# Seven block products for eight in the first MLP GEMM, with the activations of the MLP kept in DRAM and w_out run by halves of the tokens

## The chip, the cores and the metric

The kernel runs on one core of one Trainium2 chip. A core has a matrix engine (TensorE, PE in the profile; its weight loads are listed apart as PEld), three engines for elementwise work (VectorE or DVE, ScalarE or ACT, GpSimd or POOL), SyncE (SP), which here issues nearly all DMA transfers, and 16 DMA engines. The metric is the time of one execution on the device in microseconds; lower is better. A run gives several such times, and the median is used.

## The reference

One decoder layer is applied to 1024 prompt tokens and 32 decode tokens, 1056 in all. Everything ahead of the MLP (two attention-like branches and their merge) is the same before and after the change. What matters here is the end of the layer:

```python
y = (jax.nn.sigmoid(ga) * ya + jax.nn.sigmoid(gb) * yb) @ w_out
x = x + gt_m * rmsnorm(y, g_post_mix)

h2 = rmsnorm(x, g_pre_mlp) * (1 + sc_f) + sh_f
u = jnp.square(jax.nn.relu(h2 @ w_up))
x = x + gt_f * rmsnorm(u @ w_down, g_post_mlp)
```

The model width is 1024 and the MLP width 4096, so `w_up` is 1024 x 4096 and `w_down` 4096 x 1024. All values are float32, and the vectors `gt_m`, `sc_f`, `sh_f`, `gt_f` differ between the prompt and each of the 8 decode sequences.

## The kernel before, in words

All activations are kept channel-major: a tile has 128 channels on the partitions and tokens along the free axis. A float32 operand of a GEMM is split into two rounded parts, high and low, and a product is three matmuls for each block of 128 input channels: high weight x high activation, high x low, low x high (lines 400 to 402, in the helper `gemm`). They accumulate in one PSUM bank for one block of 128 output channels and one chunk of 352 tokens; three chunks make up the 1056 tokens (`CH`, line 26). Weights arrive by DMA as `wr`, and ACT makes the high part `wh` (line 261), DVE and POOL in turn the low part `wl` (line 262), for 128 x 1024 values at a time.

The last GEMM before this part is the second projection of the merge (`merge_b`). Its eviction writes the merged activations as high and low parts into `MG`, a pair of tiles for each chunk of 352 tokens.

Then `w_out` runs chunk by chunk. Each of its 8 blocks of output channels is copied out of PSUM by ACT (line 1289), squared by ACT (line 1294) and summed by POOL (line 1295). `rstd` sums over the partitions with small matmuls (line 1231) and `rstd_bc` spreads the result over all partitions with another set (line 1242), into PSUM. The norm is applied by DVE (line 1248), the residual is added by DVE and POOL in turn (line 1303; in the last chunk line 1305), the squares of the sum are added up again (line 1311), a second `rstd_bc` follows, and DVE and ACT make the high and low parts of `h2` (lines 1322 and 1323). The input `x` comes token-major from DRAM and is turned by PE (line 1279). The sum `x1` is also stored to DRAM, for the residual at the end.

The MLP goes in 8 rounds `j` of 512 hidden channels. In a round the first GEMM computes 4 blocks of `u` (8 blocks of input channels, three chunks); its eviction makes the relu and the square, in high and low parts (lines 1344 to 1347), and they stay in SBUF. The second GEMM multiplies them with 512 rows of `w_down` for all 8 blocks of output channels and adds the result to an accumulator in SBUF (line 1356). The first round follows an order written out by hand (`ORD`): chunks 0 and 1 go ahead through both GEMMs while chunk 2 still has its norms before it. The last round of the second GEMM goes chunk by chunk, each with its norm, its residual (turned back by PE) and its store.

The order of the instructions on each engine is set when the kernel is built: a scheduler takes them by their order in the program, as they become ready in its own model of time. Tiles come from pools with a fixed number of slots for each name; where a pool is closed and another one opened over the same memory, the new tiles wait for the old ones.

## Time and profile before

| | |
|---|---|
| median of three runs | 1894.65 us (1889.71 to 1897.87) |
| the profiled execution | span 1904.5 us from its first to its last instruction |
| PE busy | 1857.2 us, 98% of the span |
| PEld, DVE, ACT, POOL busy | 1754.2, 836.6, 757.5, 453.7 us |
| DMA | 180.63 MB, mean 95 GB/s |
| mean granted clock of PE | 0.979 |

The profiled execution is one more execution than those timed; its span lies 9.9 us above their median, so sums of its rows are held against its own 1904.5 us. A busy PE means that at least one matmul is in flight: matmuls overlap, and a row's duration (0.32 us for 352 columns) is longer than the distance from one start to the next (0.16 us). In the profile's rows a group is written as line, engine, operation, output tile `<-` input tiles, shapes and count; then busy time, mean of one in ns, idle time of the engine before it and what ended it.

### The profile page before, as it was taken

Reading aid. Unit: us, or ns where it says so; the run is one execution under the profiler, and the core shown is the slowest. Engines: PE = TensorE matmul, PEld = TensorE weight load, DVE = VectorE, ACT = ScalarE, POOL = GpSimd, SP = SyncE. Lnnn points to the kernel's source line nnn. Section 1 sums busy time; section 2 is a strip of 40 time slices with the busy share of each in tenths; the row PEclk is TensorE's granted clock in tenths of the full one; section 3 lists DMA queues with packets and bytes.
Section 4 is the critical chain, followed back from the end, with each engine's and each line's share of the span. In section 5 each row is a group of like instructions: output and inputs, shape, how many; then the busy total and the mean of one; then the engine's idle time right before and its main releaser. Section 6 shows DMA issues by size and latency. Waiting matters only on the chain.

```text
span 1904.5 us, 28954 instructions
## 1 busy us (share of the span) xinstructions
PE 1857.2 (98%) x11665; PEld 1754.2 (92%) x11665; DVE 836.6 (44%) x1817; ACT 757.5 (40%) x1349; POOL 453.7 (24%) x418
## 2 busy tenths in 40 slices
...
GB/s 274 78 70 60 140 91 79 56 76 107 175 175 219 74 62 58 75 210 105 86 136 117 197 120 97 111 45 45 45 45 45 45 46 55 45 45 45 45 72 122
DMA packets 207645, 180.63 MB, mean 95 GB/s; under 512 B 13108, under 2 KB 192880, under 8 KB 207512
## 3 DMA queue, kind: packets, MB, share of 16 engines
...
q8 instruction: 91, 1.49, 0.3%
...
## 4 chain that ended last, share of the span: by engine, by line
PE 90%; DMA 4%; DVE 3%; SPq 1%; issue 1%; ACT 1%; POOL 0%; DVEq 0%; POOLq 0%; ACTq 0%
PE ps_g L400 25%; PE ps_g L402 25%; PE ps_g L401 24%; PE ps_s L677 2%; PE ps_t L702 2%; PE ps_s L674 1%; PE ps_g L462 1%; DMA wr<-in_w_ada 1%; DMA Pt<-in_x_sample 1%; PE ps_s L1123 1%; PE ps_t L750 1%; PE ps_o L707 1%; PE ps_o L712 1%; PE ps_o L810 1%; PE ps_o L711 1%
## 5 line engine op out<-in xcount | busy, mean ns | idle before, releaser
L401 PE MATMUL ps_g<-Xl,wh 128*128 128x352 f32 (+1 forms) x2040 | 664.9, 326 | 0.9 <-DVE Xl L343 0.9
L400 PE MATMUL ps_g<-Xh,wh 128*128 128x352 f32 (+1 forms) x1880 | 623.5, 332 | 3.0 <-ACT Pt L1344 2.8
L402 PE MATMUL ps_g<-Xh,wl 128*128 128x352 f32 (+1 forms) x1880 | 619.8, 330 | 0.2 <-DVE wl L262 0.2
L401 PEld LDWEIGHTS ps_g<-Xl,wh 128*128 128x128 f32 (+1 forms) x2040 | 385.8, 189 | 6.9 <-issue 3.9
L400 PEld LDWEIGHTS ps_g<-Xh,wh 128*128 128x128 f32 (+1 forms) x1880 | 356.8, 190 | 9.5 <-issue 3.4
L402 PEld LDWEIGHTS ps_g<-Xh,wl 128*128 128x128 f32 (+1 forms) x1880 | 357.0, 190 | 6.4 <-issue 4.5
L262 POOL TENSOR_TENSOR wl<-wr,wh 128x1024 fp32r<-128x1024 f32 x72 | 172.9, 2401 | 721.1 <-ACT wh L261 688.0
L261 ACT CAST wh<-wr 128x1024 fp32r<-128x1024 f32 x144 | 150.9, 1048 | 441.2 <-PE ps_g L401 409.1
L1346 POOL TENSOR_TENSOR Pt<-Pt 128x352 f32<-128x352 f32 x96 | 86.3, 900 | 259.8 <-ACT Pt L1344 259.8
L262 DVE TENSOR_TENSOR wl<-wr,wh 128x1024 fp32r<-128x1024 f32 x72 | 92.1, 1279 | 126.8 <-ACT wh L261 121.1
L1344 ACT ACTIVATE Pt<-ps_g 128x352 f32<-128x352 f32 x96 | 44.3, 461 | 161.5 <-PE ps_g L402 158.6
L1356 DVE TENSOR_TENSOR Xh<-Xh,ps_g 128x352 f32<-128x352 f32 x96 | 49.9, 520 | 118.6 <-PE ps_g L402 118.6
L402 PE MATMUL ps_g<-Xl,wl 128*128 128x352 f32 x256 | 82.9, 324 | 0.0
L400 PE MATMUL ps_g<-Xl,wh 128*128 128x352 f32 x256 | 82.7, 323 | 0.0
L678 DVE CUSTOM_DVE_ANT_0 Pt<-ps_s,nF 128x384 f32<-128x384 f32 (+4 forms) x96 | 51.7, 554 | 64.0 <-PE ps_t L702 39.0
L685 ACT ACTIVATE Pt<-Pt,nm 128x128 f32<-128x128 f32 (+3 forms) x64 | 49.7, 777 | 31.3 <-DVE nm L683 20.8
L704 ACT CAST PT<-ps_t 128x512 fp32r<-128x512 f32 (+1 forms) x80 | 40.5, 545 | 52.6 <-PE ps_t L702 51.9
L705 DVE TENSOR_TENSOR PT<-ps_t,PT 128x512 fp32r<-128x512 f32 (+1 forms) x80 | 48.3, 631 | 28.3 <-ACT PT L704 28.2
L1347 DVE TENSOR_TENSOR VA<-Pt,QA 128x352 fp32r<-128x352 f32 x24 | 15.0, 625 | 93.6 <-POOL Pt L1346 93.6
L400 PE MATMUL ps_g<-QA,wh 128*128 128x352 f32 x168 | 54.5, 324 | 0.0
L402 PE MATMUL ps_g<-QB,wl 128*128 128x352 f32 x168 | 54.5, 324 | 0.0
L401 PE MATMUL ps_g<-vT,wh 128*128 128x352 f32 x168 | 54.4, 324 | 0.0
...
## 6 DMA issues: line engine op xcount, KB each, us to landing
...
```

The costliest lines, as they stand in the source:

```text
L261: act.copy(wh, wr)
L262: (dve if lo_turn[0] % 2 else pool).tensor_sub(wl, wr, f(wh))
L400: pe.matmul(o, wh[:, k], rh(k, a, b), start=(k == 0), stop=False)
L401: pe.matmul(o, wh[:, k], rl(k, a, b), start=False, stop=False)
L402: last = pe.matmul(o, wl[:, k], rh(k, a, b), start=False, stop=(k == nk - 1))
L678: dve.tensor_tensor_reduce(Pt[:, k0:k1], s_, nF[:, k0:k1], 1.0, -3.0e38, ALU.add, ALU.max, mx[:, pi:pi + 1])
L685: act.activation(Pt[:, :nk], Pt[:, :nk], AF.Exp, bias=nm, accum_out=sm)
L704: act.copy(PTh[:, :w_], pt[:, :w_])
L705: dve.tensor_sub(PTl[:, :w_], pt[:, :w_], f(PTh[:, :w_]))
L1344: act.activation(r, o, AF.Relu)
L1346: pool.tensor_tensor(u, r, r, ALU.mult)
L1356: dve.tensor_tensor(accs[a // 352](ft), accs[a // 352](ft), o, ALU.add)
```

## The change

Split `w_up` into pairs of output blocks and halves of its input channels. For pair `i`, A11 and A12 are the first and second 512 input rows for output block `2i`, and A21 and A22 the same for block `2i + 1`. Split `h2` into halves of its channels and halves of the tokens: B11, B21 for tokens 0 to 527, B12, B22 for tokens 528 to 1055. The plain way needs 8 block products of 128 output channels x 512 input channels x 528 tokens for a pair. The changed kernel uses Strassen's algorithm in the form with shared sums: M1 = A11 B11, M2 = A12 B21, and five products of combinations, of weights (`S[0]` to `S[3]`, made for each pair) and of activations (`T1` to `T4`, made once by `operands`), with A22 T4 and S[3] B22 among them. Sums of the products in PSUM, partly copied out between (`read`), give the four blocks of the result.

A product is 4 blocks of input channels x 3 matmuls x 2 pieces of 264 tokens. M1 and M2 need only the first half of the tokens: `first_two` runs them for the first `PRE = 4` pairs ahead of `operands`, with M1 kept in SBUF (`s`).

Around it: `w_out` runs by halves of the tokens, in pieces of 264 (so does the merge's second projection, which writes `MG`), and its weights are loaded once per half. The factor of a norm is copied from PSUM to SBUF (`r`). The result of the first GEMM gets its relu and square in float32 and is stored to DRAM (`d_u`); after all pairs are done, the second GEMM's rounds load it again, 4 blocks of 128 x 1056 a round, and make high and low parts (`load_u`). Weights are loaded as 1 MB pieces and split in parts of 128 x 512 (`split4`). Pools are moved so that those of the MLP lie over those of the earlier stages, and with `reuse_waits="tile"` a new tile waits only for the old ones under it. The second GEMM itself and the last chunks' norms keep their chunks of 352. Comments are dropped from the file.

```diff
-CM = 352
+TQ = 264
+CQ = tuple((a, a + TQ) for a in range(0, T, TQ))
+PRE = 4
+NPC = 6
...
-    big = ctx.enter_context(tc.tile_pool(name="big", bufs=1))
+    work = ExitStack()
+    wp = work.enter_context(tc.tile_pool(name="wp", bufs=2))
+    fp_ = work.enter_context(tc.tile_pool(name="fp", bufs=1))
+    hps = ExitStack()
+    hp = hps.enter_context(tc.tile_pool(name="hp", bufs=1, side="right"))
+    big = work.enter_context(tc.tile_pool(name="big", bufs=1))
     def slot(role, shape, dt=F32):
...
+    ms2 = ExitStack()
+    mgp = ms2.enter_context(tc.tile_pool(name="mg", bufs=1, reuse_waits="tile", side="right"))
+    yps = ExitStack()
+    yp = yps.enter_context(tc.tile_pool(name="yp", bufs=1, side="right"))
     yl = tl(op, [P, 4, T], F32R, "oT", 1)
...
+    MG = [(tl(mgp, [P, 8, TQ], F32R, "X", 8), tl(mgp, [P, 8, TQ], F32R, "X", 8)) for _ in CQ]
...
+    w2p = ctx.enter_context(tc.tile_pool(name="w2p", bufs=1, reuse_waits="tile"))
+    turn = [0]
+    def raw_w(w, k0, nk, c0, n):
+        wr = tl(w2p, [P, nk, n], F32, "raw", 3)
+        sp.dma_start(wr, w[k0 * P:(k0 + nk) * P, c0:c0 + n].rearrange("(k p) c -> p k c", p=P))
+        return wr
+    def split4(src):
+        h_ = tl(w2p, [P, 4, P], F32R, "ph", NPC)
+        l_ = tl(w2p, [P, 4, P], F32R, "pl", NPC)
+        act.copy(h_, src)
+        turn[0] += 1
+        (dve if turn[0] % 3 == 0 else pool).tensor_sub(l_, src, f(h_))
+        return h_, l_
...
+    def rstd_bc(pl, ssq, n):
+        rt = rstd(ssq, n)
+        r = tl(pl, [P, n], F32, "r", 2)
+        for c0 in range(0, n, 512):
+            c1 = min(c0 + 512, n)
+            pr = bank("s")
+            for t0 in range(c0, c1, P):
+                w_ = min(P, n - t0)
+                pe.matmul(pr[:, t0 - c0:t0 - c0 + w_], bc(rt[:w_, t0 // P:t0 // P + 1], P), ident[:w_, :w_], start=True, stop=True)
+            act.copy(r[:, c0:c1], pr[:, :c1 - c0])
...
+    TH = T // 2
+    Q = []
+    hi, lo = {}, {}
+    def xs(pl, dt=F32R):
+        return tl(pl, [P, 4, TH], dt, "X", 8 if pl is mgp else 7)
+    def part(name, x, hpl, lpl):
+        hi[name], lo[name] = xs(hpl), xs(lpl)
+        act.copy(hi[name], x)
+        dve.tensor_sub(lo[name], x, f(hi[name]))
...
+    for th in range(2):
+        a, b = th * TH, (th + 1) * TH
+        m = min(b, NP) - a
+        Q.append([xs(qp, F32) for _ in range(2)])
+        Y = lambda ft: Q[th][ft // 4][:, ft % 4]
+        ssq = sums(npl, TH)
+        for fp in range(4):
+            wr = raw_w(w_out, 0, 8, fp * 2 * P, 2 * P)
+            for ft in (2 * fp, 2 * fp + 1):
+                pieces = [split4(wr[:, 4 * kh:4 * kh + 4, (ft % 2) * P:(ft % 2 + 1) * P]) for kh in range(2)]
+                def evac(a_, b_, o):
+                    c = slice(a_ - a, b_ - a)
+                    act.copy(Y(ft)[:, c], o)
+                    if ft == 0:
+                        act.activation(ssq[:, c], o, AF.Square)
+                    else:
+                        sq = tl(npl, [P, TQ], F32, "sq", 2)
+                        act.activation(sq, o, AF.Square)
+                        pool.tensor_tensor(ssq[:, c], ssq[:, c], sq, ALU.add)
+                for a_, b_ in CQ[2 * th:2 * th + 2]:
+                    o = bank("g")[:, :TQ]
+                    for k in range(8):
+                        (wh, wl), kk = pieces[k // 4], k % 4
+                        pe.matmul(o, wh[:, kk], mg_h(k, a_, b_), start=(k == 0), stop=False)
+                        pe.matmul(o, wh[:, kk], mg_l(k, a_, b_), start=False, stop=False)
+                        pe.matmul(o, wl[:, kk], mg_h(k, a_, b_), start=False, stop=(k == 7))
+                    evac(a_, b_, o)
...
+        xT = [xs(mgp if th else qp, F32) for _ in range(2)]
+        for t0, t1 in tok_tiles(a, b):
             w_ = t1 - t0
+            for q in range(2):
+                xt = tl(w2p, [P, 512], F32, "S", 4)
+                for r0, r1, src in dram_rows(x_p, x_s, t0, t1):
+                    sp.dma_start(xt[r0:r1], src[:, q * 512:(q + 1) * 512])
+                pt = bank("t").rearrange("p (a b) -> p a b", b=P)
+                for k in range(4):
+                    pe.transpose(pt[:, k, :w_], xt[:w_, k * P:(k + 1) * P], ident[:w_, :w_])
+                act.copy(xT[q][:, :, t0 - a:t1 - a], pt[:, :, :w_])
+        r = rstd_bc(npl, ssq, TH)
+        ssq2 = sums(npl, TH)
         for ft in range(8):
+            y = Y(ft)
+            scaled(y, r, gt_m, ft, m, TH)
+            (pool if ft % 2 else dve).tensor_tensor(y, y, xT[ft // 4][:, ft % 4], ALU.add)
+            if ft == 0:
+                act.activation(ssq2[:, :TH], y, AF.Square)
+            else:
+                sq = tl(npl, [P, TH], F32, "sq2", 2)
+                act.activation(sq, y, AF.Square)
+                (dve if ft % 2 else pool).tensor_tensor(ssq2[:, :TH], ssq2[:, :TH], sq, ALU.add)
+            if ft % 4 == 3:
+                sp.dma_start(d_x1[:, ft - 3:ft + 1, a:b], Q[th][ft // 4])
+        r2 = rstd_bc(npl, ssq2, TH)
+        for ft in range(8):
+            y = Y(ft)
+            scaled(y, r2, a_f, ft, m, TH)
+            act.activation(y[:, :m], y[:, :m], AF.Identity, bias=sh_f[:, ft, 0:1])
+            if m < TH:
+                per_seq(y, y, sh_f, ft, m, TH, ALU.add)
+        if th == 0:
+            for kq in range(2):
+                part(kq, Q[0][kq], qp, mgp)
+    nps.close()
...
+    def operands():
+        (B11, B21), (B12, B22) = Q
+        t3 = xs(qp, F32)
+        pool.tensor_tensor(t3, B22, B12, ALU.subtract)
+        dve.tensor_tensor(B12, B12, B11, ALU.subtract)
+        dve.tensor_tensor(B11, B22, B12, ALU.subtract)
+        dve.tensor_tensor(B21, B21, B11, ALU.subtract)
+        part("T2", B11, mgp, mgp)
+        part("T1", B12, mgp, mgp)
+        part("T4", B21, mgp, mgp)
+        part("T3", t3, qp, qp)
+        part("B22", B22, qp, qp)
+    stg = ExitStack()
...
+    def product(accs_, w, x, first):
+        wh, wl = w
+        for (s0, s1), acc in zip(SUB, accs_):
+            o = acc[:, :TQ]
+            for k in range(4):
+                pe.matmul(o, wh[:, k], hi[x][:, k, s0:s1], start=first and k == 0, stop=False, skip_group_check=True)
+                pe.matmul(o, wh[:, k], lo[x][:, k, s0:s1], start=False, stop=False, skip_group_check=True)
+                pe.matmul(o, wl[:, k], hi[x][:, k, s0:s1], start=False, stop=k == 3, skip_group_check=True)
+    def u_out(c, ft, th):
+        act.activation(c, c, AF.Relu)
+        act.activation(c, c, AF.Square)
+        sp.dma_start(d_u[ft, :, th * TH:(th + 1) * TH], c)
+    def first_two(i):
+        wr = raw_w(w_up, 0, 8, 2 * i * P, P)
+        A11, A12 = split4(wr[:, 0:4]), split4(wr[:, 4:8])
+        ab, bb = [bank8() for _ in SUB], [bank8() for _ in SUB]
+        s = tl(sgp, [P, TH], F32, "s", PRE)
+        c11 = tl(sgp, [P, TH], F32, "c", 3)
+        product(ab, A11, 0, True)
+        for (s0, s1), acc in zip(SUB, ab):
+            act.copy(s[:, s0:s1], acc[:, :TQ])
+        product(bb, A12, 1, True)
+        for (s0, s1), acc in zip(SUB, bb):
+            dve.tensor_tensor(c11[:, s0:s1], acc[:, :TQ], s[:, s0:s1], ALU.add)
+        u_out(c11, 2 * i, 0)
+        return s
+    def pair(i, s=None):
+        wr = raw_w(w_up, 0, 8, 2 * i * P, 2 * P)
+        a11, a12, a21, a22 = wr[:, 0:4, 0:P], wr[:, 4:8, 0:P], wr[:, 0:4, P:], wr[:, 4:8, P:]
+        S = [tl(w2p, [P, 4, P], F32, "S", 4) for _ in range(4)]
+        dve.tensor_tensor(S[0], a21, a22, ALU.add)
+        dve.tensor_tensor(S[1], S[0], a11, ALU.subtract)
+        dve.tensor_tensor(S[2], a11, a21, ALU.subtract)
+        dve.tensor_tensor(S[3], a12, S[1], ALU.subtract)
+        ab = [bank8() for _ in SUB]
+        tiles = {}
+        def read(what):
+            for n_, ((s0, s1), acc) in enumerate(zip(SUB, ab)):
+                t = tl(sgp, [P, TQ], F32, "v", 4)
+                tiles[what, n_] = t
+                if pre:
+                    dve.tensor_tensor(t, acc[:, :TQ], s[:, s0:s1], ALU.add)
                 else:
+                    act.copy(t, acc[:, :TQ])
+        def add(c, what, bb):
+            for n_, ((s0, s1), acc) in enumerate(zip(SUB, bb)):
+                dve.tensor_tensor(c[:, s0:s1], acc[:, :TQ], tiles[what, n_], ALU.add)
+        quad = lambda: tl(sgp, [P, TH], F32, "c", 3)
+        pre = s is not None
+        if not pre:
+            product(ab, split4(a11), 0, True)
+            read("M1")
+            bb = [bank8() for _ in SUB]
+            product(bb, split4(a12), 1, True)
+            c11 = quad()
+            add(c11, "M1", bb)
+            u_out(c11, 2 * i, 0)
+        product(ab, split4(S[1]), "T2", pre)
+        read("U2")
+        db = [bank8() for _ in SUB]
+        product(db, split4(S[0]), "T1", True)
+        product(ab, split4(S[2]), "T3", False)
+        read("U3")
+        c22 = quad()
+        add(c22, "U3", db)
+        u_out(c22, 2 * i + 1, 1)
+        product(ab, split4(a22), "T4", False)
+        c21 = quad()
+        for (s0, s1), acc in zip(SUB, ab):
+            if pre:
+                dve.tensor_tensor(c21[:, s0:s1], acc[:, :TQ], s[:, s0:s1], ALU.add)
             else:
+                act.copy(c21[:, s0:s1], acc[:, :TQ])
+        u_out(c21, 2 * i + 1, 0)
+        product(db, split4(S[3]), "B22", False)
+        c12 = quad()
+        add(c12, "U2", db)
+        u_out(c12, 2 * i, 1)
+    kept = [first_two(i) for i in range(PRE)]
+    operands()
+    for i in range(FF // (2 * P)):
+        pair(i, kept[i] if i < PRE else None)
+    stg.close()
+    qps.close()
+    ms2.close()
+    _mark(nc, "down")
     FC = 4
     NJ = FF // (FC * P)
+    dnp = ctx.enter_context(tc.tile_pool(name="dnp", bufs=1, reuse_waits="tile"))
+    xw = ctx.enter_context(tc.tile_pool(name="xw", bufs=1, reuse_waits="tile", side="right"))
+    def trio(tag):
+        t = [tl(dnp, [P, T], F32, tag, 8).rearrange("p (a b) -> p a b", b=352) for _ in range(3)]
...
+    def load_u(j):
+        out = []
+        for i in range(FC):
+            lt = tl(dnp, [P, T], F32R, "ul", 8)
+            ht = tl(dnp, [P, T], F32R, "uh", 8)
+            sp.dma_start(f(lt), d_u[j * FC + i])
+            act.copy(ht, f(lt))
+            (dve if i % 2 else pool).tensor_sub(lt, f(lt), f(ht))
+            out.append((ht, lt))
+        return (lambda k, a, b: out[k][0][:, a:b]), (lambda k, a, b: out[k][1][:, a:b])
+    acc_t = [tl(xw, [P, 8, 352], F32, f"acc{c}", 1) for c in range(3)]
...
+        for q in range(2):
+            wr = raw_w(w_dn, j * FC, FC, q * 512, 512)
+            for c in range(4):
+                if j < NJ - 1:
+                    gemm(split4(wr[:, :, c * P:(c + 1) * P]), FC, u_h, u_l, down_evac(4 * q + c))
+                else:
+                    d_h = tl(xw, [P, FC, P], F32R, f"dh{4 * q + c}", 1)
+                    d_l = tl(xw, [P, FC, P], F32R, f"dl{4 * q + c}", 1)
+                    act.copy(d_h, wr[:, :, c * P:(c + 1) * P])
+                    dve.tensor_sub(d_l, wr[:, :, c * P:(c + 1) * P], f(d_h))
+                    wd.append((d_h, d_l))
...
+    def load_x1(a, b):
+        t = [tl(dnp, [P, T], F32, "uh", 8).rearrange("p (a b) -> p a b", b=352) for _ in range(3)]
+        for i, n_ in enumerate((3, 3, 2)):
+            sp.dma_start(t[i][:, 0:n_], d_x1[:, 3 * i:3 * i + n_, a:b])
+        return lambda ft: t[ft // 3][:, ft % 3]
```

228 lines of the change are left out of this document (63 added, 165 removed).

## The prediction

> **What bounds the kernel now.** I read the page's engine shares first, then its chain, then the busy time by stretches of the MLP part.
>
> ```profile
> span 1904.5 us, 28954 instructions
> PE 1857.2 (98%) x11665; PEld 1754.2 (92%) x11665; DVE 836.6 (44%) x1817; ACT 757.5 (40%) x1349; POOL 453.7 (24%) x418
> PE 90%; DMA 4%; DVE 3%; SPq 1%; issue 1%; ACT 1%; POOL 0%; DVEq 0%; POOLq 0%; ACTq 0%
> 1016.50:1190.00 173.50, 166.15 (x1055) 164.31 (x1054) 102.98 (x183) 90.82 (x179) 93.69 (x74) 0.98 0.45 136
> 1190.00:1830.00 640.00, 640.00 (x3964) 639.81 (x3963) 154.65 (x259) 146.95 (x246) 147.78 (x117) 1.00 0.17 51
> 1830.00:1904.50 74.50, 66.82 (x453) 64.94 (x451) 48.26 (x92) 25.99 (x49) 27.55 (x28) 0.95 0.33 112
> ```
>
> The stretches give time, PE, PEld, DVE, ACT and POOL busy with their counts, granted clock, DMA share and GB/s. PE is the path (90% of the chain). From 1190 to 1830 PE never pauses, while DVE, ACT and POOL each work a quarter of the time and DMA moves 51 GB/s. So a matmul less is time less there: 640.00 / 3964 = 0.1615 us for each matmul of 352 columns. From 1016.5 to 1190 stand w_out, the norms and the first MLP rounds; there DVE, ACT and POOL are busy 52 to 59% and PE loses 173.50 - 166.15 = 7.4 us idle, and 2% of clock, 3.5 us.
>
> **Matmul price at 264 columns.** The first GEMM has 32 blocks x 8 k x 3 x 3 chunks = 2304 matmuls of 352 columns. After: 16 pairs x 7 products x 4 k x 3 x 2 = 2688 of 264. No row has 264; its neighbours are 256 and 272.
>
> ```profile
> 201.68 0.28 PE L711 MATMUL ps_o<-PT,VB 128*128 128x256 f32 x1
> 201.80 0.27 PE L712 MATMUL ps_o<-PT,VB 128*128 128x256 f32 x1
> 201.91 0.28 PE L707 MATMUL ps_o<-PT,VB 128*128 128x256 f32 x1
> 202.03 0.28 PE L710 MATMUL ps_o<-PT,VB 128*128 128x256 f32 x1
> 202.15 0.28 PE L711 MATMUL ps_o<-PT,VB 128*128 128x256 f32 x1
> 202.27 0.28 PE L712 MATMUL ps_o<-PT,VB 128*128 128x256 f32 x1
> ...
> 514.14 0.29 PE L760 MATMUL ps_s<-u,u 128*64 128x272 f32 x1
> 514.26 0.29 PE L758 MATMUL ps_s<-Pt,raw 128*128 128x272 f32 x1
> 514.39 0.29 PE L760 MATMUL ps_s<-u,u 128*64 128x272 f32 x1
> ```
>
> From start to start: 256 columns (202.27 - 201.68) / 5 = 0.118 us, 272 columns 0.125. So 264 costs 0.122, nearly in proportion to 352; bounds 0.118 and 0.125. The new weights loaded for every matmul don't set it: the 256-wide ones change weights each time too. First GEMM: 2304 x 0.1615 = 372.1 to 2688 x 0.122 = 327.9, **-44** (-55 to -36). The second projection of the merge and w_out go from 288 + 576 matmuls of 352 (139.5) to 384 + 768 of 264 (140.5): **+1**. The second GEMM keeps its 2304 matmuls of 352. The old losses before 1190 belong to an order of chunks that goes: **-11**. Without new stalls that is -54.
>
> **The hand-over at the second token half.** This is the largest new cost. A column of products can use the second half (T1 to T4, B22) only after both norms of that half, five subtractions over 128x2112 and the high and low parts. Between the last w_out matmul and product T2, PE has only first_two: 4 x 2 products x 24 x 0.122 = 23.4 us, and about 2.5 of small matmuls. The chain is priced from the second chunk's norm on DVE (start, time, count in the timeline; the last two rows are the third chunk's):
>
> ```profile
> 1096.81 0.15 DVE L1232 TENSOR_SCALAR rv<-ps_o 128x3 f32<-128x3 f32 x1
> ...
> 1099.54 1.23 DVE L262 TENSOR_TENSOR wl<-wr,wh 128x1024 fp32r<-128x1024 f32 x1 [0.35 <-ACT wh L261]
> ...
> 1101.86 1.55 DVE L1248 SCALAR_TENSOR_TENSOR KB<-KB,mod,ps_s 128x352 f32<-128x352 f32 x3
> ...
> 1104.82 1.06 DVE L1248 SCALAR_TENSOR_TENSOR nF<-nF,mod,ps_s 128x352 f32<-128x352 f32 x2
> 1105.80 2.08 DVE L1303 TENSOR_TENSOR KB<-KB,Pt 128x352 f32<-128x352 f32 x2
> 1107.81 1.26 DVE L1303 TENSOR_TENSOR stg<-stg,Pt 128x352 f32<-128x352 f32 x1
> ...
> 1121.64 0.15 DVE L1232 TENSOR_SCALAR rv<-ps_o 128x3 f32<-128x3 f32 x1
> ...
> 1128.11 1.07 DVE L1248 SCALAR_TENSOR_TENSOR h2f<-KB,mod,ps_s 128x352 f32<-128x352 f32 x2 [0.33 <-PE ps_s L1242]
> ...
> 1168.97 0.16 DVE L1232 TENSOR_SCALAR rv<-ps_o 128x3 f32<-128x3 f32 x1 [1.44 <-PE ps_o L1231]
> ...
> 1172.45 0.55 DVE L1248 SCALAR_TENSOR_TENSOR h2f<-Xh,mod,ps_s 128x320 f32<-128x320 f32 x1 [2.46 <-PE ps_s L1242]
> ```
>
> Two rows of the timeline for ACT, and groups by form for POOL (busy, mean ns):
>
> ```profile
> 1054.34 0.45 ACT L1289 COPY KB<-ps_g 128x352 f32<-128x352 f32 x1
> 1058.35 1.05 ACT L261 CAST wh<-wr 128x1024 fp32r<-128x1024 f32 x1 [3.20 <-POOL rt L1233]
> ```
>
> ```profile
> L1303 POOL TENSOR_TENSOR KB<-KB,Pt 128x352 f32<-128x352 f32 x1 | 1.0, 952 | 1.4 <-DVE KB L1248 1.4
> L1303 POOL TENSOR_TENSOR stg<-stg,Pt 128x352 f32<-128x352 f32 x2 | 2.5, 1226 | 0.0
> L262 POOL TENSOR_TENSOR wl<-wr,wh 128x1024 fp32r<-128x1024 f32 x15 | 35.8, 2389 | 29.5 <-ACT wh L261 29.4
> ```
>
> 1. The last eviction (two ACT operations at 0.4, a POOL sum at 0.8, waits): 2.5 us.
> 2. Statistics to first scaling: 5.1 (1096.81 to 1101.86) and 6.5 (1121.64 to 1128.11) now. The sums on PE stand before that, and the copies to SBUF are new: 6 us, twice.
> 3. First scaling, residual, squares: 19.8 us (1101.86 to 1121.64) for 352 columns. At 528 a DVE operation grows from 0.49 between starts to 0.67 and one of POOL from 0.95 to 1.33 (slopes between the 352 and 1024 rows), 1.38 times: 27; the two weight parts of 1024 columns in that stretch become smaller ones: 24.
> 4. Second scaling of 8 blocks, 0.67 + 0.3 for decode tokens: 8.
> 5. Operands: POOL makes T3's difference before DVE may overwrite B12. 2112 columns extrapolate to 4.75 on POOL, 2.3 on DVE, 2.0 on ACT: 4.75 + 2 x 2.3 + 2.0 + 2.3 = 13.7.
>
> Sum 60, so PE waits 60 - 26 = **+34**. Low end: statistics 4 twice (3.5 in the third chunk, 1168.97 to 1172.45) and 18 for step 3 give 50, wait 24; high end, with half 0's leftover in front, 72, wait 45. The row pair at L1303 POOL (0.95 alone, 1.23 while DVE runs the same form, whose 1.26 stands beside 0.49) is why I take 24 and not the 18 that the operations add up to.
>
> The Trainium skill, "SBUF — State Buffer", section "Who interferes with whom", says that a DVE instruction with two SBUF inputs and a reading GpSimd instruction exclude each other. By that rule, which these rows bear out, scaling also collides after the change, since its factor then comes from SBUF and not from PSUM; were there no such rule, step 3 would be 18 and the wait 28.
>
> After a wait that long the clock falls, as these stretches near the start show (the granted clock stands third from the end):
>
> ```profile
> 48.00:55.00 7.00, 0.68 (x3) 0.50 (x4) 1.49 (x5) 0.00 (x0) 0.00 (x0) 0.72 0.68 164
> 55.00:61.70 6.70, 6.06 (x34) 4.68 (x32) 6.18 (x13) 5.98 (x11) 2.08 (x3) 0.78 0.82 203
> 61.70:68.50 6.80, 6.38 (x43) 5.63 (x44) 6.00 (x19) 5.02 (x8) 0.00 (x0) 1.00 0.01 3
> ```
>
> After the 7 us at 48 it recovers by 61.7. The loss is (1 - 0.72) x 7 + (1 - 0.78) x 6.7 = 3.4 us, of which part fell into the idle time: **+3** (0 to 4). The Trainium skill, "TensorE: Matmul & The Clock Gate", Part 1, The HAM clock gate, has the clock at half after an idle window of 3.4 us until one busy window has passed. The trace agrees; by that rule alone the loss would be about 1.7 us, as an estimate, and the sum a microsecond lower. It speaks against any edit that lets PE pause.
>
> The remaining parts (T1, T4, T3, B22) follow 2.3 us apart while DVE also reads banks; T3, used third, is made fourth: **+2** (0 to 4).
>
> **Other edits.** The first half's chain (2.5 + 6 + 24 + 6 + 5.4 without decode columns, and 5 for its two pairs of parts: 49) has 46.8 of w_out's second half and 5 of transposes over it: 0, with the leftover counted above; its cover gone, up to 10. The first w_out weights take slots of the merge's last ones: a cast and a subtraction of 512 columns after it, **+2** (0 to 4). In the steady pairs PE needs 7 x 24 x 0.122 = 20.5 us; ACT has 7 casts of 512 (0.6), 8 bank copies (0.4) and 8 squares or relus (0.6), 12.2 us; DVE 4 differences and 2 or 3 low parts of 512 columns (0.65) and 6 bank sums (0.4), 6.8; POOL 5 low parts at 1.3. All lies under PE. DMA gets 1.05 MB of weights and 1.08 MB of stores in 20.5 us, 104 GB/s, below the 164 and 203 seen above. A read of a bank between T3 and T4 has 1.5 us of PE over it: **+1** for all pairs (0 to 6). SP issues 4 stores and a load a pair, hidden by the same.
>
> At the start of the second GEMM four blocks of 0.54 MB come from DRAM into memory that products held until the end; loads queue on SP behind the last stores. Two late blocks at 203 GB/s are 5.3 us, then a cast of 1.1 and a POOL difference of 2.4, less the matmuls that the early blocks feed and the 2.9 of the last product: **+6** (2 if all have space early, 16 if all four come late). The later rounds have 46 us each over 10.7 of loads. The last chunks' weights, norm and transposes stay; their buffers are fewer: **+1** (-2 to +6).
>
> **Sum.** -44 + 1 - 11 + 34 + 3 + 2 + 2 + 1 + 6 + 1 = -5. The span goes from 1904.5 to 1899.5; that execution lies 9.9 above the median 1894.65 of the runs, so I predict **1890**.
>
> **Rivals.**
> - *The cover holds better* (PE waits 10 to 22): the chain needs only its own operations since POOL and DVE have little else then. For it: 18 by the bare operations; the 3.5 us that the third chunk's statistics take. Against: two chunks now take 19.8. A wait of 22 gives 1890 - 12 = 1878, one of 10 with 8 less for the clock and the small terms 1858; the middle wait of 16 gives 1872. Chance 0.30.
> - *The chains saturate DVE and POOL*: slower. Half 0's chain ends late, first_two starts late, and half 1's follows it. It decides from 52 us on, what w_out's second half covers; if both chains take 1.25 times my price, 61 and 75, PE waits 10 + 49 where I counted 34: 1890 + 25 = 1915; at 1.15 times (56 and 69) 1903. For it: DVE and POOL between 1016.5 and 1190 are already busy 59 and 54% with two SBUF users; against: PE idles only 7.4 there. Chance 0.15.
> - *The second GEMM waits for DRAM*: if loads start only after the last store has landed, the last block's sum, relu and square (0.4 + 0.6 + 0.6), 3 for its store and 10.7 of four loads, 1.1 and 2.4 stand bare: 19 for 6, and a clock loss of 3: 1906. Against it: the store read first is 300 us old. Chance 0.09.
>
> **Numbers.** The forecast case (waits of 24 to 45) has 0.46 and its own range 1878 to 1904. Faster than 1885.2 is 0.30 + 0.07 of the forecast case = 0.37; slower than 1904.1 is 0.15 + 0.09 = 0.24; within 0.5%, which is what a measurement here can't tell from nothing, 0.39. The range 1866 to 1911 takes in the matmul's bounds and leaves out the ends of the cover and saturation cases.
>
> **What would show it.** A 264-wide matmul at 0.122 between starts in the products; a pause of PE of 25 to 45 us between the last first_two product and T2, ended by DVE's low part of T2; one of 2 to 10 us at the first use of u, ended by the cast or POOL; DVE, ACT and POOL below 70% in the pairs. I am wrong if that first pause is under 20 or over 50, if pairs take over 22 us, or if time is lost before the merge.

## The result, and the profile after

The changed kernel takes **1949.26 us** (median of four runs, 1937.38 to 1950.82) against 1894.85 us for the kernel before on the same chip (1889.71 to 1897.87): a ratio of **1.0271 [1.0234, 1.0308]**, slower. The prediction was 1890 us with a range up to 1911, so it missed the size and the sign. The profiled execution of the changed kernel took 1948.05 us, close to its median. All the runs told of below were in the fast state but one execution of e9 (3817.87 us), which its figures leave out.

The page of the changed kernel: span, engine shares, and PE's busy share in 40 slices of 48.7 us each.

```profile
span 1946.3 us, 30982 instructions
PE 1831.2 (94%) x12353; PEld 1723.1 (89%) x12353; DVE 907.5 (47%) x1907; ACT 860.6 (44%) x1553; POOL 491.5 (25%) x436
PE   6899999999999999999999494899999899999998
```

PE was busy in 98% of the span before, now in 94%. Nearly all of the loss is in three slices: 1070 to 1120, 1168 to 1217, and a little at 1540. The same by stretches from the last matmul of the merge to the end (the merge is the stage ahead of `w_out`; columns as in the prediction: time, then PE, PEld, DVE, ACT, POOL busy with counts, granted clock, DMA share, GB/s). Before:

```profile
1016.50:1904.50 888.00, 872.97 (x5468) 869.06 (x5466) 305.89 (x534) 263.76 (x472) 269.02 (x218) 0.99 0.24 73
```

And after:

```profile
1018.70:1946.30 927.60, 844.72 (x6064) 836.83 (x6064) 373.64 (x609) 367.82 (x672) 307.26 (x230) 0.95 0.31 104
...
1025.00:1090.00 65.00, 64.09 (x520) 63.36 (x520) 11.64 (x16) 29.11 (x67) 34.38 (x33) 0.98 0.47 155
1090.00:1125.00 35.00, 9.01 (x40) 8.39 (x41) 20.18 (x21) 18.26 (x29) 11.72 (x10) 0.54 0.24 86
1125.00:1162.00 37.00, 37.00 (x301) 37.00 (x301) 2.77 (x4) 15.09 (x37) 20.09 (x21) 0.97 0.25 70
1162.00:1233.00 71.00, 39.87 (x271) 37.93 (x269) 46.60 (x90) 33.05 (x58) 29.39 (x18) 0.76 0.29 96
1233.00:1537.80 304.80, 304.80 (x2490) 304.65 (x2490) 116.29 (x205) 168.04 (x319) 89.91 (x69) 0.99 0.33 107
1537.80:1548.00 10.20, 1.31 (x4) 0.79 (x3) 2.31 (x3) 5.48 (x8) 3.10 (x4) 0.60 0.91 333
1548.00:1946.30 398.30, 388.49 (x2445) 384.56 (x2445) 172.55 (x270) 97.14 (x155) 117.37 (x75) 0.98 0.26 92
```

The tail grew by 927.60 - 888.00 = 39.6 us, where the prediction's terms add up to -5. It splits into PE's idle time, (927.60 - 844.72) - (888.00 - 872.97) = **+67.9**, and its busy time, 844.72 - 872.97 = **-28.2**. The idle time stands in two stretches, 1090 to 1125 (26.0 of 35.0) and 1162 to 1233 (31.1 of 71.0), and at 1537.8 (8.9); smaller ones stand at 1024.9 (6.2) and in the second GEMM. In the steady pairs, 1233 to 1537.8, PE never pauses and 304.80 / 2490 = 0.1224 us is the price of a 264-wide matmul.

PE's waits in that part, as the profile puts them down (who waits, for whom: us in total, times, longest):

```profile
PE ps_o L1261 <- DVE ssq L1361: 33.2, 2, 19.8
PE ps_g L1335 <- ACT ssq L1325: 10.8, 1, 10.8
PE ps_g L404 <- ACT uh L1518: 7.7, 1, 7.7
PE ps_g L1335 <- ACT ph L1233: 6.2, 1, 6.2
PE ps_g L1410 <- ACT s L1428: 4.1, 1, 4.1
PE ps_g L1410 <- ACT X L1307: 2.8, 1, 2.8
PE ps_g L1411 <- DVE X L1308: 2.3, 1, 2.3
```

The two longest are not where the prediction put its pause. PE's own timeline (start, time, instruction, and the idle time before it) places them; ACT's, below it, shows what ends the pause before 1121.52.

```profile
1104.26 2.29 PE L1261 MATMUL ps_o<-u,ssq 128*128 128x1 f32 x10 [13.36 <-DVE ssq L1361]
...
1121.52 0.59 PE L1335 MATMUL ps_g<-X,ph 128*128 128x264 f32 x1 [10.84 <-ACT ssq L1325]
...
1195.05 2.29 PE L1261 MATMUL ps_o<-u,ssq 128*128 128x1 f32 x10 [19.82 <-DVE ssq L1361]
...
1227.29 0.51 PE L1410 MATMUL ps_g<-X,ph 128*128 128x264 f32 x2 [2.77 <-ACT X L1307]
```

```profile
1118.94 1.95 ACT L1307 CAST X<-X 128x2112 fp32r<-128x2112 f32 x1
1120.80 0.37 ACT L1323 COPY X<-ps_g 128x264 f32<-128x264 f32 x1
1121.07 0.39 ACT L1325 ACTIVATE ssq<-ps_g 128x264 f32<-128x264 f32 x1
```

**First half.** The matmuls at L1261 add up the squares for the second norm of token half 0. They stand in PE's queue ahead of 312 of the 384 `w_out` matmuls of half 1, which need nothing of that norm. PE stops at them for 13.4 us, does them, and stops again for 10.8: its next `w_out` block needs a bank, and the copy and the square that empty one (L1323 at 1120.80, then L1325) stand in ACT's queue behind the first half's squares, biases and casts of 2112 columns. So `w_out` of half 1 did not cover the first half's chain; all but 72 of its matmuls came after it.

**Second half.** Between the last `w_out` matmul (1161.9) and T2 (1227.3) pass 65.4 us. PE's largest pause in it, 19.8, again stands ahead of the second statistics: products of `first_two` are queued behind them.

Last, the clock. The three longest stretches at half clock, all around pauses, with the granted clock third from the end:

```profile
1092.70:1126.90 34.20, 10.28 (x44) 9.87 (x45) 17.48 (x19) 17.62 (x28) 10.30 (x9) 0.50 0.18 68
1178.10:1202.00 23.90, 6.70 (x30) 6.61 (x30) 11.66 (x23) 5.65 (x9) 13.86 (x9) 0.50 0.38 134
1539.90:1553.50 13.60, 6.71 (x22) 6.26 (x23) 6.32 (x3) 7.84 (x9) 7.75 (x3) 0.50 0.93 358
```

Of these 71.7 us PE was busy for 23.7, so about 12 us of its work was time lost to the half clock. They are not the only ones: 1024.9 to 1028.0, 1208.9 to 1215.6 and 1229.5 to 1236.1 also have 0.50 to 0.52. In all, PE's busy time multiplied by what was missing from the granted clock, in slices of 2 us, gives an estimate of 18.7 us lost in this tail and 4.1 in that of the kernel before, 14.6 more. That is why the busy time fell by 28.2 and not by the 43 that fewer matmuls give.

### The profile page after: what moved, and what is told of

The parts are those of the page before. It is cut to its first block, busy times and chain, and to the rows that moved or that the text cites. A ratio compares the mean times of both kernels' runs of the same rounds, so it can differ in the third digit from the quotient of the medians.

```text
span 1946.3 us, 30982 instructions
## 1 busy us (share of the span) xinstructions
PE 1831.2 (94%) x12353; PEld 1723.1 (89%) x12353; DVE 907.5 (47%) x1907; ACT 860.6 (44%) x1553; POOL 491.5 (25%) x436
## 5 line engine op out<-in xcount | busy, mean ns | idle before, releaser
L404 PE MATMUL ps_g<-Xh,wh 128*128 128x352 f32 (+1 forms) x1176 | 393.7, 335 | 1.5 <-ACT wh L265 1.4
L406 PE MATMUL ps_g<-Xh,wl 128*128 128x352 f32 (+1 forms) x1176 | 390.4, 333 | 0.0
L405 PE MATMUL ps_g<-Xl,wh 128*128 128x352 f32 (+1 forms) x1080 | 356.7, 330 | 0.4 <-DVE Xl L347 0.4
L404 PEld LDWEIGHTS ps_g<-Xh,wh 128*128 128x128 f32 (+1 forms) x1176 | 222.7, 189 | 8.0 <-issue 3.0
L406 PEld LDWEIGHTS ps_g<-Xh,wl 128*128 128x128 f32 (+1 forms) x1176 | 221.8, 189 | 6.2 <-issue 4.2
L404 PE MATMUL ps_g<-uh,ph 128*128 128x352 f32 x672 | 218.0, 326 | 8.4 <-ACT uh L1518 7.7
L405 PE MATMUL ps_g<-ul,ph 128*128 128x352 f32 x672 | 216.8, 323 | 1.3 <-POOL ul L1519 1.3
L406 PE MATMUL ps_g<-uh,pl 128*128 128x352 f32 x672 | 216.5, 322 | 0.0
L405 PEld LDWEIGHTS ps_g<-Xl,wh 128*128 128x128 f32 (+1 forms) x1080 | 204.0, 189 | 5.9 <-issue 3.9
L1410 PE MATMUL ps_g<-X,ph 128*128 128x264 f32 x340 | 98.4, 290 | 6.9 <-ACT s L1428 4.1
L1411 PE MATMUL ps_g<-X,ph 128*128 128x264 f32 x340 | 98.8, 291 | 2.3 <-DVE X L1308 2.3
L1335 PE MATMUL ps_g<-X,ph 128*128 128x264 f32 x256 | 75.2, 294 | 17.0 <-ACT ssq L1325 10.8
```

Of the source, the lines that this page charges most:

```text
L404: pe.matmul(o, wh[:, k], rh(k, a, b), start=(k == 0), stop=False)
L405: pe.matmul(o, wh[:, k], rl(k, a, b), start=False, stop=False)
L406: last = pe.matmul(o, wl[:, k], rh(k, a, b), start=False, stop=(k == nk - 1))
L1335: pe.matmul(o, wh[:, kk], mg_h(k, a_, b_), start=(k == 0), stop=False)
L1410: pe.matmul(o, wh[:, k], hi[x][:, k, s0:s1], start=first and k == 0, stop=False, skip_group_check=True)
L1411: pe.matmul(o, wh[:, k], lo[x][:, k, s0:s1], start=False, stop=False, skip_group_check=True)
```

## The experiments

My theory after the result: the loss is one of order and length of two chains of elementwise work, half 0's because PE's and ACT's queues put it ahead of independent `w_out` work, half 1's because it is longer than what PE has to do meanwhile. The rivals: the chains are late for want of DVE and POOL time in any order; or the buffers of the products, which lie on memory of the norms, hold the products back. Each experiment is compared with the kernel before on its own chip. "Tail" is the profile's time from the merge's last matmul to the end (927.7 in the changed kernel), "chain" the time from the last `w_out` matmul to T2's first (65.4).

### e1: half 0's chain woven into w_out of half 1

```diff
+W0 = {0: 1, 1: 1, 2: 1, 3: 1, 4: 1, 5: 1, 6: 1, 7: 1, 8: 1, 9: 1, 11: 1, 12: 1, 13: 3, 14: 3, 15: 2}
...
+    def norms(th, xT, ssq):
...
+            two[ft % 2].tensor_tensor(y, y, xT[ft // 4][:, ft % 4], ALU.add)
...
+            yield
...
-                    evac(a_, b_, o)
+                    ev = evac(a_, b_, o)
+                    if th:
+                        advance(0, W0.get(unit, 0), (last, ev))
```

The norms become a generator. After each piece of `w_out` of half 1, some of its steps are issued, tied behind that piece's last matmul and its square. No operation is added or taken away.

> The first token half's norm chain is issued step by step behind the chunks of the second half's w_out (its statistics matmuls on PE and its copies and squares on ACT queue behind the chunk's last matmul and last square), nothing else is changed. Theory 1 (order of the queues: 312 of the second half's 384 w_out matmuls stood behind the first half's second statistics): the pauses of 13.6, 1.9 and 11.2 us around 1090 to 1121 go, w_out's second half runs through in about 47 us, and with the clock lost after them the time falls by 26 to 31 us, to 1918 to 1923. Theory 2 (the first half's chain saturates DVE and POOL, so w_out's second half would wait for its low parts and its sums anyway): the pauses come back as many small ones on PE ended by POOL pl or ACT ph, and the time falls by less than 10 us.

Measured: 1922.42 us against 1899.39, ratio **1.0132 [1.0088, 1.0177]**, tail 904.3. Against the changed kernel's ratio of 1.0271 this is 1.4%, 26 us, as expected of the order; the tail is 23.4 us shorter. The stretches of `w_out` and of half 1's chain in this kernel:

```profile
1020.40:1126.00 105.60, 105.60 (x850) 104.86 (x851) 37.34 (x37) 54.84 (x126) 70.06 (x63) 0.97 0.41 134
1126.00:1199.20 73.20, 39.05 (x274) 36.93 (x271) 47.45 (x90) 34.95 (x61) 31.26 (x17) 0.81 0.34 108
```

All of `w_out` now runs in 105.6 us without a gap (137 in the changed kernel, 1024.9 to 1161.9), and the pauses of 13.4, 1.5 and 10.8 are gone. DVE and POOL had the time; for half 0 the order was the cause. The chain of half 1 grew from 65.4 to 73.2.

### e2: buffers of the products off the memory of the norms

```diff
-    nps.close()
-
-    stg = ExitStack()
-    sgp = stg.enter_context(tc.tile_pool(name="sgp", bufs=1, reuse_waits="tile"))
...
-                sq = tl(npl, [P, TH], F32, "sq2", 2)
+                sq = tl(npl, [P, TH], F32, "c", CB)
...
-        s = tl(sgp, [P, TH], F32, "s", PRE)
-        c11 = tl(sgp, [P, TH], F32, "c", 3)
+        s = tl(npl, [P, TH], F32, "s", PRE)
+        c11 = tl(npl, [P, TH], F32, "c", CB)
...
-        wr = tl(w2p, [P, nk, n], F32, "raw", 3)
+        wr = tl(w2p, [P, nk, n], F32, "raw", 2)
```

Only `s` gets memory that the norms never use; `c` and `v` take turns in the same slots with `r` and the squares of the norms.

> The buffers of the first MLP products (s, c, v) no longer lie on the memory of the norms (ssq, r, squares): they are cut from one pool with them; the raw weights keep 2 buffers for 3. No order is given. Theory 1a (first_two could run only 96 of its 192 matmuls before the second half's chain ended, since its first copies to s waited until 1209.8 for memory that the norms held): these copies come within a few us of their matmuls, all of first_two's matmuls run ahead of the operands, and the pauses of the second half (20.1, 4.4, 3.0 and 4.0, in all 31.5) shrink by the 11.7 us of the other 96 matmuls, to about 20; the time falls by 8 to 14 us, to 1935 to 1941. Theory 2a (the copies were late because ACT had the chain's work in front of them, not for the memory): no change within 3 us. The first half's pauses stay as they are in both.

Measured: 1944.48 us, **1.0236 [1.0191, 1.0280]**, tail 931.1; no difference from the changed kernel is established, where 1935 to 1941 was expected. The first copy of M1 out of its bank, in the changed kernel and here:

```profile
1209.79 0.64 ACT L1428 COPY s<-ps_g 128x264 f32<-128x264 f32 x2
```

```profile
1155.47 0.38 ACT L1468 COPY s<-ps_g 128x264 f32<-128x264 f32 x1 [0.75 <-PE ps_g L1450]
```

That is 3 us after the last `w_out` matmul (1152.4) for 48 in the changed kernel (1161.9), so memory did hold these copies back. Yet nothing is won: PE's pauses around that half only move (16.4, 4.5, 11.4 and about 1 us in small ones, 34 together, for 31). What has to end is the chain, and when `first_two` is done PE waits for it just the same.

### e3: both, and half 1's chain woven into first_two

```diff
+W1 = {0: 1, 1: 1, 2: 2, 3: 2, 4: 2, 5: 2, 7: 1}
...
-        product(bb, A12, 1, True)
+        last = product(bb, A12, 1, True)
...
-        u_out(c11, 2 * i, 0)
+        ev = u_out(c11, 2 * i, 0)
+        advance(1, W1.get(2 * i + 1, 0), (last, ev))
```

> The two edits together, and the second half's chain is issued behind first_two's products in the same way. Theory 1 with 1a: both savings add up, 34 to 45 us less than the changed kernel, 1904 to 1915; one pause of some 20 us is left ahead of T2, as long as the chain's 48 us less 23.4 of first_two and the transposes. Theory 2: above 1930.

Measured: 1924.03 us, **1.0123 [1.0074, 1.0172]**, tail 902.7: as e1, and not the 1904 to 1915 expected. The stretch of half 1's chain:

```profile
1128.50:1204.00 75.50, 37.14 (x273) 35.43 (x271) 53.19 (x93) 36.23 (x64) 33.07 (x18) 0.77 0.34 107
```

The chain takes 75.5 us and PE has 37 us of work in it, at a clock of 0.77; its pauses (0.6, 2.4, 4.7, 9.6, 1.5 and 19.6) add up to 38. For this half this order alone does not help. The chain even grew; DVE and POOL also make sums and low parts for the coming pairs in it, but that this is why it grew is not shown.

### e4: the adds of the chain all on DVE

```diff
-            (pool if ft % 2 else dve).tensor_tensor(y, y, xT[ft // 4][:, ft % 4], ALU.add)
+            dve.tensor_tensor(y, y, xT[ft // 4][:, ft % 4], ALU.add)
...
-                (dve if ft % 2 else pool).tensor_tensor(ssq2[:, :TH], ssq2[:, :TH], sq, ALU.add)
+                dve.tensor_tensor(ssq2[:, :TH], ssq2[:, :TH], sq, ALU.add)
```

The order is that of the changed kernel.

> In the norm chains of both halves the residual adds and the sums of squares are all on DVE, none on POOL; the order is the changed kernel's own. Theory 1 (a DVE instruction with two SBUF inputs takes 1.8 us for 0.7 beside one of POOL's, and sums that alternate between the engines cost 2.2 us a pair of steps): a step of the chain becomes 3 x 0.68 = 2.0 us on DVE, 16 for the eight instead of the 20 of now, so each half's pause shrinks by about 4 us and the time falls by 6 to 10 us. Theory 2 (DVE's own work is the limit and POOL's share was a relief): each chain grows by 5 us or more and the time rises by 8 or more.

Measured: 1938.11 us, **1.0221 [1.0180, 1.0262]**, tail 920.6. The ratio is 0.5% below the changed kernel's, with intervals that overlap; the tail is 7.1 us shorter, where 6 to 10 were expected. DVE's timeline of half 0 (scalings, residuals, sums of squares), in the changed kernel, where POOL makes half of the residuals and sums, and here, where DVE makes all:

```profile
1084.76 7.60 DVE L1286 SCALAR_TENSOR_TENSOR X<-X,mod,r 128x528 f32<-128x528 f32 x8
1092.28 4.76 DVE L1355 TENSOR_TENSOR X<-X,X 128x528 f32<-128x528 f32 x4
```

```profile
1075.91 5.52 DVE L1292 SCALAR_TENSOR_TENSOR X<-X,mod,r 128x528 f32<-128x528 f32 x8
1081.34 5.03 DVE L1330 TENSOR_TENSOR X<-X,X 128x528 f32<-128x528 f32 x8
1086.29 5.57 DVE L1336 TENSOR_TENSOR ssq<-ssq,sq 128x528 f32<-128x528 f32 x7
```

Eight scalings take 5.52 us here and 7.60 beside POOL's residuals; eight residuals take 5.03 and four took 4.76. All of it is done in 16.0 us by one engine, from 1075.91 to 1091.86; two engines needed 19.5, from 1084.76 to PE's 1104.26. PE's pauses before the second statistics fell from 13.4 and 19.8 to 10.0 and 16.2. So POOL's help makes the chain longer. The Trainium skill, "SBUF — State Buffer", section "Who interferes with whom", has the rule that a DVE instruction with two SBUF inputs contends with a GpSimd instruction that reads SBUF. The trace agrees, and this is its price here, 3.4 and 3.6 us in the two halves.

### e5: eight pairs of cover for four

```diff
-PRE = 4
+PRE = 8
+SPILL = 4
...
+        if i < SPILL:
+            sp.dma_start(d_s[i], s)
...
+    def back(i):
+
+        s = tl(npl, [P, TH], F32, "s", 4)
+        sp.dma_start(s, d_s[i])
+        return s
```

On top of e3: M1 and M2 run ahead for eight pairs; four of the kept M1 go through DRAM, and the pairs whose M1 stayed are finished first.

> As the experiment with both edits, but eight pairs' first two products for four stand between w_out and T2 (four of their M1 tiles go to DRAM and come back); the second half's chain is issued behind them, its second statistics behind the twelfth product. Theory 1b (the second half's chain takes 66 to 71 us from the last w_out matmul to T2 and needs only cover): PE has 47 us of products for 23.4, the pauses of that half fall from 38 us to 10 to 20, and the time lies 18 to 28 us below the kernel with both edits: 1896 to 1906 where the kernel before takes 1899. Theory 2b (the products' own weight pieces and evictions on DVE, POOL and ACT make the chain longer, about as much as they cover): pauses stay above 28 us, the time falls by less than 10.

Measured: 1902.96 us against 1894.99, **1.0045 [1.0016, 1.0074]**, tail 885.7; 0.8% or 15 us less than e3, where 18 to 28 were expected. The same stretch here:

```profile
1126.30:1210.40 84.10, 58.44 (x465) 57.10 (x463) 56.95 (x104) 46.43 (x88) 38.77 (x23) 0.87 0.46 147
```

PE has 58.4 us of work in the chain for 37.1, but the chain grew from 75.5 to 84.1 and a pause of 22.2 is left. The longer cover brings its own evictions: DVE is busy for 57.0 us in the chain for 53.2, ACT for 46.4 for 36.2. That they are what delays it fits, but was not tested alone.

### e6: earlier starts of w_out and of the second GEMM

```diff
+    first = [pieces_()]
...
+    def last_pair(i):
...
+        product(eb, split4(S[3]), "B22", True)
+        product(ab, split4(a11), 0, True)
...
+        product(ab, split4(S[1]), "T2", False)
...
+        u_out(c22, 2 * i + 1, 1, act)
```

On top of e1, on the memory layout of e2: the first pair of split weights is allocated ahead of the raw weights, which moves these to memory that the merge gives up earlier; the last pair runs its products in another order and stores from ACT's queue, so that `u` need not queue behind the stores. T3's parts are made last.

> As the kernel with the first half's chain behind the chunks of w_out, with three edits at the two starts: the raw w_out weights lie on memory that the merge gives up before its end; the last pair takes its products in the order B22, M1, T2, T1, T3, T4, M2, so that the memory for the first blocks of u comes free 6 to 17 us before the end; the last pair's stores are issued by ACT, so that the loads of u stand behind no store on SP. Theory 1c (the 6.5 us at w_out's start is the load that can't be issued before the merge's last matmul; the 9.7 us at the second GEMM's start are loads behind the last two stores, plus 1.8 and half clock): the first pause falls below 2, the second below 3, and the time by 12 to 18 us, to 1904 to 1910. Theory 2c (the loads are held by the transfers themselves or by casts and subtractions on ACT and POOL): the pauses fall by less than a half, the time by less than 6.

Measured: 1911.38 us, **1.0087 [1.0052, 1.0122]**, tail 898.0: 0.45% or 9 us below e1, where 12 to 18 were expected. The intervals overlap; the tail is 6.3 us shorter. PE's waits at the two starts:

```profile
PE ps_g L409 <- ACT uh L1604: 5.2, 1, 5.2
...
PE ps_g L1397 <- ACT ph L1242: 2.6, 1, 2.6
```

The pause at the start of `w_out` fell from 6.4 in e1 to 2.6, that of the second GEMM from 8.8 to 5.2. In the changed kernel SP's queue shows what stands ahead of the loads of `u`: three stores, then all eight loads behind them, the first from 1540.64.

```profile
1534.87 5.68 SPq L1417 DMA_DIRECT2D d_u<-c  x3
1540.64 3.96 SPq L1517 DMA_DIRECT2D ul<-d_u  x8
```

### e7: e1 to e6 together

```diff
-PRE = 4
+PRE = 8
...
-CHAIN = 'both'
+CHAIN = 'dve'
...
-        pool.tensor_tensor(t3, B22, B12, ALU.subtract)
+        dve.tensor_tensor(t3, B22, B12, ALU.subtract)
...
+        with tc.issue_after(gate.ins) if n_ < 4 else nullcontext():
```

On top of e6; the pairs' weight sums also wait behind the operands.

> All edits together: both chains behind the matmuls, eight pairs of first products, the chains' adds and T3's difference on DVE, the weight sums of the pairs behind the operands' first difference on DVE, and the edits at the two starts. If each saving is its own (1b 18 to 28, 1c 12 to 18, the adds on DVE 4 to 8 from the second half alone), the time is 1922 less 4 of own memory less these: 1866 to 1886, below the kernel before (1899). If a common limit stands behind them (DVE and POOL, or the clock after any pause), it stays above 1895.

Measured: 1900.05 us, **1.0046 [1.0010, 1.0082]**, tail 889.5, where 1866 to 1886 was expected. The chain:

```profile
1110.30:1193.20 82.90, 61.38 (x466) 60.25 (x463) 52.85 (x104) 44.08 (x83) 18.43 (x12) 0.84 0.41 137
```

It is still 82.9 us, and PE waits 18.5 us ahead of T2 and 2.6 and 1.8 right behind its start. The gains do not add. DVE now carries the chain's adds, the evictions of the cover and the differences, yet it is busy for only 52.9 of the 82.9 us, so want of DVE time alone does not explain the chain's length.

### e8: a shorter chain by order

```diff
+                    if th and unit == XU:
+                        xT = x_turned(1)
...
+            with tc.issue_after(res[ft - 2].ins) if ft > 1 else nullcontext():
+                scaled(y, r, gt_m, ft, m, TH)
...
+        t1 = xs(mgp, F32)
+        dve.tensor_tensor(t1, B12, B11, ALU.subtract)
+        dve.tensor_tensor(B11, B22, t1, ALU.subtract)
```

On top of e7: the transposes of `x` go among the `w_out` pieces, scalings keep two ahead of the residuals, T1's difference gets its own tile so that T2 need not wait for T3, and T4's comes last. Raw weights load in two transfers each.

> As the kernel with all edits, with the second half's chain shortened by order alone: the transposes of x stand among w_out's chunks, so that PE reaches the first statistics' spread 8 us sooner; on DVE the scaling of a block waits for the residual two blocks back, so that the squares start after the first block and not after the eighth (9 us); T1's difference gets a tile of its own, so that T2's is ready one operation of 2.36 us after the last scaled block, and T4's difference and the weight sums stand behind the low parts of T2 and T1 (5 us). The first w_out weights come in two transfers, the second weights of the second GEMM stand behind the first loads of u. Theory 1d (the chain of 75 us is mostly waiting on orders): it falls to about 53, the pause ahead of T2 from 18.8 + 3.0 + 2.2 to below 6, the one at the second GEMM from 5.2 + 1.8 to below 3, and the time by 18 to 28 us against the kernel with all edits, to 1872 to 1882 where the kernel before takes 1895. Theory 2d (DVE's own work sets the chain): the pauses stay above 14 in all and the time above 1890.

Measured: 1896.45 us against 1902.55, **0.9978 [0.9948, 1.0008]**, tail 880.6, where 1872 to 1882 was expected. The chain is 72.7 us, ten less than in e7 by order alone, and the pause ahead of T2 14.2. The whole chain, and a stretch from its middle:

```profile
1127.30:1200.00 72.70, 54.90 (x425) 54.16 (x424) 56.50 (x105) 42.14 (x77) 21.89 (x15) 0.87 0.48 155
...
1145.00:1172.50 27.50, 27.50 (x227) 27.47 (x227) 26.39 (x52) 16.73 (x35) 7.22 (x5) 1.00 0.76 246
```

In the middle DVE is busy for 26.39 of 27.50 us (96%): there its work is the chain's limit. Over the whole chain it is busy for 56.5 of 72.7, so orders still have a part.

### e9: eight products for seven, all else as in e8

```diff
-        hi["T3"], lo["T3"] = xs(qp), xs(qp)
...
-        part("T4", B21, mgp, mgp)
+        gate = part("B12", B12, mgp, mgp)
...
+    def quarter(w0, x0, w1, x1, ft, th, hook=None, q=None):
...
+        last = both(acc, w0, x0, True, False)
...
+        last = both(acc, w1, x1, False, True)
```

> The kernel with the shortened chain, but with eight block products for seven: each quarter of the result is one accumulation of two products in PSUM, no differences of weights or operands, no sums of banks, nothing kept of the first products. If the seventh-for-eighth product is worth what its matmuls cost (16 pairs x 24 x 0.122 = 46.9 us), this takes 40 to 48 us more than the kernel with seven. If Strassen's sums on DVE, POOL and the kept products eat half of it, below 25 more.

Measured: 1919.64 us (median of five), **1.0127 [1.0068, 1.0186]**, tail 904.7. That is 1.5%, 28 us by the ratios, more than e8; the medians give 23 and the tails 24. It is below the 40 to 48 expected if the seven products saved all of their matmuls' cost. The stretch of the whole first GEMM:

```profile
1128.00:1513.20 385.20, 381.46 (x3112) 380.53 (x3112) 58.96 (x105) 191.71 (x361) 75.72 (x59) 1.00 0.34 113
```

The 384 matmuls more cost 384 x 0.1224 = 47 us by themselves. The plain form saves the 14.2 us ahead of T2 and all differences and bank sums (DVE is busy for 59 us in the whole stretch). So in this layout Strassen's form is worth about 23 to 28 us net: an eighth of the matmuls saved, less the operands it needs first.

### e10: work taken off DVE

```diff
-        product(bb, A12, 1, True)
-        for (s0, s1), acc in zip(SUB, bb):
-            dve.tensor_tensor(c11[:, s0:s1], acc[:, :TQ], s[:, s0:s1], ALU.add)
+        last = product(ab, A12, 1, False)
+        for (s0, s1), acc in zip(SUB, ab):
+            act.activation(c11[:, s0:s1], acc[:, :TQ], AF.Relu)
```

On top of e8: M1 is copied out and M2 accumulates on it in the same bank, so the sum in `first_two` costs DVE nothing and ACT takes the relu from the bank; the statistics get earlier places in the weave, the loads of `x` are paced, `first_two` takes its banks and its pairs in another order, and the last pair makes T1's product later.

> As the kernel with the shortened chain, which still needed 70 us from the last w_out matmul to T2, with DVE busy for nearly all of the 27 us of residuals and squares. The first products' sums leave DVE: the second product is accumulated onto the first's bank once that is copied out, and ACT takes the relu from the bank. The first half's second statistics stand two chunks earlier, the second half's after the eleventh product, its second scaling waits for no square of a product on ACT; x's token tiles are turned two chunks apart; the last pair takes T3 and T4 ahead of T1. Theory 1e (DVE's 5 us of sums, the first half's late parts and the orders on ACT make the rest): the chain falls to 50 to 58 us, the pause of 14.4 ahead of T2 below 5, the 4.1 and 1.8 at the second GEMM below 2, and the time by 15 to 24 us, to a ratio of 0.985 to 0.990 to the kernel before. Theory 2e (what a step costs on DVE beside POOL's weight pieces sets the chain): the pause stays above 10, the ratio above 0.994.

Measured: **1882.36 us against 1903.93, 0.9895 [0.9842, 0.9949]**, tail 865.1: 1% under the kernel before, with an interval below 1, and 3.7% below the changed kernel. The stretch of the chain, and then PE's longest waits in this kernel:

```profile
1134.60:1196.40 61.80, 52.36 (x425) 51.43 (x423) 47.20 (x87) 39.87 (x85) 21.20 (x16) 0.96 0.56 182
```

```profile
PE ps_g L1490 <- ACT X L1329: 8.6, 1, 8.6
PE ps_g L411 <- ACT uh L1669: 3.8, 1, 3.8
PE ps_g L1433 <- ACT ph L1248: 2.6, 1, 2.6
```

The chain is down to 61.8 us with 52.4 of PE work in it and the clock back at 0.96. Three pauses over 2 us remain, the longest still ahead of T2. DVE is busy in the chain for 47.2 us after 56.5 in e8. The ratio came as expected, but the chain (50 to 58), the pause ahead of T2 (under 5) and that at the second GEMM (under 2) did not. Several orders changed together with DVE's work, so what the relief of DVE gives alone is not shown.

### e11 and e12: both kernels once more

The unchanged kernels, each profiled a second time, to see how far the split of the time ahead of the merge and after it holds.

> The kernel before, unchanged, profiled a second time. Its profiled execution lay 11 us above its median and had 37.5 us at half clock from 894 to 932 without a pause of PE before it; the changed kernel's did not. Theory 1f (that stretch belongs to the one execution): here the merge ends 10 to 20 us earlier than at 1016.5, and the rest after it takes 888 us again, within 3. So the change costs the 40 us that the two traces show behind the merge, and the other 12 to 14 between the medians come from what lies ahead of it. Theory 2f (the stretch is the kernel's own): the merge ends at 1012 to 1020 again.

> The changed kernel, unchanged, profiled a second time beside it. In all theories the time is 1.023 to 1.031 of the kernel before, what follows the merge takes 925 to 931 us, and the pauses of PE behind the merge are the same to 0.5 us. Theory 1f: the merge's end lies 5 to 15 us behind that of the kernel before in the same call. Theory 2f: at the same time, within 5.

Measured: the kernel before 1896.38 us (0.9985 [0.9959, 1.0010] of its other runs), tail 892.3 after 887.8; the changed kernel 1941.09 against 1899.78, **1.0258 [1.0206, 1.0311]**, tail 930.4 after 927.7, with each pause within 1.6 us of the first profile's. The change costs (927.7 + 930.4 - 887.8 - 892.3) / 2 = **39 us** in the tail. The tail of the kernel before missed its expected 888 within 3, and the pauses their 0.5 us.

The time up to the merge scatters: 1016.7 and 1005.7 us for the kernel before, 1018.7 and 1002.8 for the changed one, so e11's merge ended 11 us earlier than in the first profile, as theory 1f had it, but e12's did not end 5 to 15 us behind e11's: it ended 3 ahead. The first profile of the kernel before has a long stretch at half clock there; the second has 3.5 us of it (900.7 to 904.2) at the matching place (first and second profile):

```profile
894.20:931.70 37.50, 37.50 (x132) 32.86 (x132) 10.59 (x42) 3.66 (x10) 5.25 (x5) 0.50 0.19 57
```

```profile
900.70:938.20 37.50, 37.50 (x227) 32.95 (x225) 18.73 (x60) 6.25 (x15) 6.75 (x6) 0.95 0.33 98
```

The second profile has a stretch of 16 us at 0.50 elsewhere (232 to 248). In slices of 2 us as above, the clock cost PE 31, 20, 27 and 13 us ahead of the merge's end in the four profiles (before, e11, after, e12). Without that the times are 985, 986, 992 and 990: most of the scatter is the clock's, and the changed kernel has some 5 us more there. What they are, no run here tells. The medians differ by 54 and 41 us in the two comparisons (51 and 49 by the ratios), 2 to 15 us beyond the tail's 39.

## Why the prediction was wrong

By its own terms, against the tail's +39.6 for -5:

- **Matmul price and first GEMM: right.** 0.122 predicted, 0.1224 measured, no pause in the steady pairs, DVE 38%, ACT 55%, POOL 29% there. The -44 and +1 hold.
- **"The first half's chain ... 49 has 46.8 of w_out's second half and 5 of transposes over it: 0": this step failed.** The length was right (1073.0 to 1123.3, 50 us), but the cover was taken as work that PE can do at any time. In PE's queue the second statistics stood ahead of 312 of the 384 covering matmuls, and in ACT's the evictions stood behind the chain. Cost 13.4 + 1.5 + 10.8 = 25.7 us; the "up to 10" given for a missing cover was too small by the same mistake. e1, which changes the order alone, took these pauses away and 26 us with them.
- **Hand-over at the second half, +34: near in size, partly by luck, and wrong in place.** PE's idle time there is 30.7 us, 27.4 of it ahead of T2. The chain was priced at 60 and took 65.4; PE's work in it was counted as 26 and took 38.0, some 6 of them lost to the clock. The two errors offset each other. DVE's rows give its parts:

```profile
1172.97 0.73 DVE L1286 SCALAR_TENSOR_TENSOR X<-X,mod,r 128x496 f32<-128x496 f32 x1
...
1203.02 0.73 DVE L1286 SCALAR_TENSOR_TENSOR X<-X,mod,r 128x496 f32<-128x496 f32 x1
...
1217.51 3.43 DVE L1384 TENSOR_TENSOR X<-X,X 128x2112 f32<-128x2112 f32 x1 [4.23 <-POOL X L1383]
```

  Eviction and first statistics took 11.1 (1161.9 to 1172.97) for 8.5; scaling to sums 22.1 (to 1195.05) for 24; second statistics 8.0 (to 1203.02), at half clock, for 6; second scaling 9.7 for 8 and operands 14.6 (1212.7 to 1227.3) for 13.7. The 24 taken for DVE and POOL in each other's way, and not 18, was the right choice, as e4 shows. But the pause was foretold as one, ahead of T2 and ended by T2's low part. 19.8 us of it stands ahead of the second statistics and only 2.3 is ended by that low part: again the place in PE's queue. Right ahead of T2 PE waits 2.8 us, where under 20 was to show the prediction wrong.
- **Clock, +3: mis-sized.** It was counted for one pause, and the old 3.5 us of clock loss were counted as gone. There are six stretches at half clock around pauses up to 1553.5, and 18.7 us are lost in the tail for the 4.1 of before, 14.6 more where the terms have about none (+3 and -3.5).
- **w_out start, +2:** 6.2. **Second GEMM, +6:** 7.7 + 1.3 = 9.0, for the reason given (loads behind the last stores); the rival with 19 us did not occur.
- **T3 order, the last chunks and the steady pairs:** no pause over 2 us in any of them, as predicted.

Together: 25.7 + 4.2 + 3.0 - 3.3 = 29.6 us more idle time than forecast, and some 15 more of clock; that is the 45 us between -5 and +39.6. Of the other 15 us of the miss against 1949, 9.9 were subtracted because the profiled execution of before lay above its median; e11 shows that these stood ahead of the merge and come and go between executions. Another 2 lie ahead of the merge in the two first profiles, and by 3 the changed kernel's span lies under its median. A tail of +39.6 put on the median of before would have given about 1934.

Of the rivals, the one that DVE and POOL saturate came nearest in time (1915), but not for its reason: in the changed kernel DVE has time in the chain (46.60 of 71.0 us busy), and e1 recovers half 0 with the same work. In part of the chain DVE is saturated once the order is mended (e8); e10 takes work off it and gains, though not by that alone.

What was not settled: how e10's gain splits between DVE's work and the orders, why the pauses at the starts of `w_out` and the second GEMM do not fall below 2.6 and 3.8 us in e10, and the 2 to 15 us above that are not in the tail. That a chain with fewer operands first (T1's and T3's products later) would close the last 8.6 us was not tried.
